# Sixteen places for the weight parts of the feed-forward layers, in tiles from the layers' own pools, with four smaller edits

## The chip, the core and the metric

The kernel runs on one core of a Trainium2 chip. The metric is the device time of one execution in microseconds (us); lower is better. TensorE (PE) multiplies, VectorE (DVE), ScalarE (ACT) and GpSimd (POOL) do the elementwise work, and SyncE (SP) issues nearly all DMAs.

## The reference, cut to what matters

A two-layer decoder trunk over 272 positions (16 learned ones and a sequence of 256), width 2048, in float32:

```python
for i in range(DEPTH):                       # 2 layers
    hn = rmsnorm(h, norm_mix[i])
    mix = mixer_ab(hn, ...) if i % 2 == 0 else mixer_cd(hn, ...)
    h = h + mix
    h = h + conv_ffn(rmsnorm(h, norm_ffn[i]), ffn_w_up[i], ffn_dw[i], ffn_w_down[i])
return rmsnorm(h, norm_final)[:, N_META:]

def mixer_ab(h, ...):
    a_val, a_gate, s_b, s_c, s_x = jnp.split(h @ w_in, ...)      # five parts, 1024 wide each
    a = silu(layernorm(causal_dwconv(a_val * sigmoid(a_gate), conf_dw) + conf_dw_b, ...))
    s = s_b * causal_dwconv(s_c * s_x, sc_dw)
    return jnp.concatenate([a, s], axis=-1) @ w_out

def conv_ffn(h, w_up, dw, w_down):           # D_FF = 5632
    u = causal_dwconv(h @ w_up, dw)          # width 3, over 2 * 5632 channels
    val, gate = u[..., :D_FF], u[..., D_FF:]
    return (jax.nn.silu(gate) * val) @ w_down
```

`mixer_cd` (gated linear attention and an RWKV-7 recurrence) is not touched by the change.

## The kernel before, in words

**Layout.** Channels lie on the 128 partitions and positions along the free axis, so the residual stream is 16 tiles `h[m]` of 128x272. A product with a weight matrix goes by output block: 128 output channels, the sum over k in steps of 128 input channels, in one PSUM tile.

**Split products.** Float32 products are made of rounded halves (type fp32r). For each group of `SUB = 4` steps of k, ACT casts the weights from the DMA'd tile `wf` to `wh` (L161), and DVE subtracts to give the rest, `wl` (L163). Then each k has three matmuls: `wh` with the high half of the moving operand (L181), `wh` with its low half (L182), `wl` with the high half (L183). In feed-forward layer 1 the up products work on 258 positions and use three forms of 260, 256 and 258 columns (L174 to L178). One output block of an up product has 16 steps of k, so 48 matmuls and four pairs of `wh` and `wl`; one of a down product, which is done in two halves of the 44 inner blocks, has 22 steps, so 66 matmuls. `wh` and `wl` are tiles of 128x512 elements, 2048 bytes per partition, in the pool `wpool`, five of each; since every tile of that pool is a multiple of 512 bytes long, all of them begin at the same remainder of 512 bytes. The moving operands have fixed places too: the normed input lies in `xslab` (`x`) and a second slab (`lt`), each half in a slot of `XW = 320` elements, where `make_x` writes them (L225 and L226), except ahead of `mixer_cd`, where the slots are 272 elements wide and so begin at several remainders of 256 bytes.

**Order.** A scheduler places the instructions of each engine from the order of the code and the tiles' dependences; the engines then run independently. A tile of a pool is free again when its last reader is done. The pools of the stages (`ab`, `ffn0`, `cd`, `ffn1`) are opened one after the other in the same memory.

**Between a mixer and its feed-forward layer.** Ahead of `ffn` the last products of the mixer are added to `h[m]` (`add_h`, L266), `make_x` writes the halves of the layer's input, and `feed` adds the squares into `nacc` (for the last block ACT squares, L240, and DVE adds, L241). `finish` sums `nacc` over the channels with a matmul against ones (L251) and gives 1/rms, `rstd`. The layer's products need only the halves, not `rstd`, which is multiplied in afterwards.

**The mixer of layer 0.** Its input product gives 40 blocks. Block triples of the short convolution part end in `sb = acc * rstd * cv`, whose halves are the moving operand `s_split` of `ab_out_s`; the last triple is ready only after the last block of the input product. Sums of squares `sums` give the mixer's `rstd`. A generator `ln_gen` gives the layer norm of the other part, a piece after each output block of `ab_out_s`.

**Start and end.** Two small constants for layer 1, `omm` and `omka`, are made by DVE (L1060, L1061). At the end 16 blocks `ob` are scaled (eleven by DVE from PSUM, five by POOL) and written out in eleven DMAs, all issued by SP (L1097).

Of the kernel before, what the change touches and what calls it, by code (L numbers as in the profile page):

```python
# [17 lines left out]
P = 128  # L18
# [4 lines left out]
KD = D // P  # L23
# [72 lines left out]
def _body(ctx, tc, nc, A):  # L96
# [53 lines left out]

    def gemm_steps(w, g, xs, kt, acc, pool_lo=(), load=LOADK):
        for k0 in range(0, kt, load):
# [3 lines left out]
            for s0 in range(0, nk, SUB):  # L156
                ns = min(SUB, nk - s0)
                src = wf[:, s0 * P:(s0 + ns) * P]
                wh = wpool.tile([P, SUB * P], F32R, tag="wh", name="wh")
                wl = wpool.tile([P, SUB * P], F32R, tag="wl", name="wl")  # L160
                last_hi[0] = S.copy(wh[:, :ns * P], src)  # L161
# [23 lines left out]

    def gemm(w, g, xs, n, pool_lo=()):
        acc = psA.tile([P, T], F32, tag="acc", name="acc")
        for _ in gemm_steps(w, g, xs, len(xs), acc[:, :n], pool_lo):
            tick()
        return acc[:, :n]  # L190
# [84 lines left out]
    def mixer_ab(tp):  # L275
# [79 lines left out]
        for i in range(8):  # L355
            ps3 = []
            for _ in range(3):
                ps3.append(gemm(A["ab_in"], g, xs, T, PLO))
                g += 1
                run_taps(NT)  # L360
                if len(ps3) == 1:
                    u = tp.tile([P, T], F32, tag="u0", name="u")
                    V.tensor_mul(u, ps3[0], nm.rstd)
                elif len(ps3) == 2:
                    u2 = tp.tile([P, T], F32, tag="u1", name="u2")
                    V.tensor_mul(u2, ps3[1], nm.rstd)
                    up = tp.tile([P, T + 2], F32, tag="up", name="up")
                    V.memset(up[:, 0:2], 0.0)
                    V.tensor_mul(up[:, 2:T + 2], u, u2)
                    cv = tp.tile([P, T], F32, tag="t2", name="cv")  # L370
                    conv3(cv, up, T, "sc_dw", i)
            sb = tp.tile([P, T], F32, tag="t3", name="sb")
            V.tensor_mul(sb, ps3[2], nm.rstd)
            V.tensor_mul(sb, sb, cv)
            d = halves[:, i]
            split(d, sb, T)
            s_split.append(parts(d, 0, T))
# [6 lines left out]
        def ln_gen():  # L384
# [5 lines left out]
            for i in range(8):  # L390
# [5 lines left out]
                if i % 2:  # L396
                    yield
            pv = psb()
            PE.matmul(pv[:, :T], ones, csum, start=True, stop=True)
# [13 lines left out]
        ln = ln_gen()  # L413
        next(ln, None)
        for m in range(KD):
            acc = gemm(A["ab_out_s"], m, s_split, T)
            h[m] = hpool.tile([P, T], F32, tag="h", name="h")
# [13 lines left out]
    def ffn(layer, nm, gname, c1, tp, feed, spill=None):  # L431
# [9 lines left out]
        for half in range(2):  # L441
            act = []
            for j in range(NFH):
                i = half * NFH + j
                res = []
                for q in range(2):
                    ps = gemm(up, 2 * i + q, xs, n + ex)
                    nm.finish()
# [15 lines left out]
            for m in range(KD):  # L464
                add_h(m, gemm(down, half * KD + m, act, no), T - no)
                if half:
# [592 lines left out]
    omka = cpool.tile([P, 16], F32, name="omka")[:, :8]  # L1059
    V.tensor_scalar(omm, par[:, PO["mu"]:PO["mu"] + 26], -1.0, 1.0, op0=ALU.mult, op1=ALU.add)  # L1060
    V.tensor_scalar(omka, par[:, PO["ka"]:PO["ka"] + 8], -1.0, 1.0, op0=ALU.mult, op1=ALU.add)  # L1061
    with tc.tile_pool(name="cd", bufs=2) as tp:
        nm = mixer_cd(tp, nm)
    with tc.tile_pool(name="ffn1", bufs=2) as tp:
# [25 lines left out]
        S.copy(rs, ps[:, :SEQ])  # L1090
        for a, b in ((0, 1), (1, 2), (11, 12), (2, 4), (12, 13), (4, 6), (13, 14), (6, 8), (14, 15), (8, 11), (15, 16)):
            for m in range(a, b):
                if m < 11:
                    V.tensor_mul(ob[:, m], ob[:, m], ps[:, :SEQ])
                else:
                    G.tensor_mul(ob[:, m], ob[:, m], rs)
            nc.sync.dma_start(A["outT"][:, a:b], ob[:, a:b])  # L1097

# [86 lines left out]
```

## Time and profile before

| | |
|---|---|
| time, median of 3 runs | 2460.76 us (2458.37 to 2470.93) |
| profiled execution, its own time | 2459.09 us |
| its span (first to last instruction) | 2457.3 us |
| PE busy | 2427.9 us, 99% of the span |
| DVE, ACT, POOL busy | 1794.0, 1338.9, 571.6 us |
| mean granted clock of TensorE | 0.997 of full speed |
| DMA | 423.95 MB, 173 GB/s over the span |

The span is measured on the chip by the profiler; the profiled execution's own time is 1.8 us longer and 1.7 us below the median of the timed runs. The stages follow one another: the mixer of layer 0 ends at about 348 us, feed-forward layer 0 at about 1130, the mixer of layer 1 at about 1701, and feed-forward layer 1 at about 2443 us. Matmuls are pipelined and overlap in the records: one has a duration of 0.28 us, but the next starts 0.12 us after it, so the distance from start to start (here called the spacing) is what a matmul costs while PE waits for nothing.

### The profile page before, as it was taken

How to read it: one execution, taken by the hardware profiler on the slowest of the kernel's cores; microseconds unless marked ns; L12 is line 12 of the kernel's file. 1: busy time of each engine (PE TensorE's matmuls, PEld its weight loads, DVE VectorE, ACT ScalarE, POOL GpSimd, SP SyncE). 2: the span in 40 equal slices, each digit the busy share in tenths (PEclk: the TensorE clock that was granted, in tenths of full speed). 3: DMA queues.
4: the chain of work that ended last, by engine and by line, in shares of the span. 5: the costliest groups of instructions: out<-in, count | busy, mean ns of one | idle time of the engine just before them, and what ended most of it. 6: DMA issues, size and time to landing. Idle time of an engine off the chain costs nothing.

```text
span 2457.3 us, 53575 instructions
## 1 busy us (share of the span) xinstructions
PE 2427.9 (99%) x20476; PEld 2371.8 (97%) x20476; DVE 1794.0 (73%) x3400; ACT 1338.9 (54%) x2573; POOL 571.6 (23%) x894
## 2 busy tenths in 40 slices
PE   8999999999999999999999999999999999999998
PEld 8999999999999999999999988899999999999997
DVE  8897897776556777667786678879777755777754
ACT  5444665555445555546745445546555545555653
POOL 5776140000000000121248044416110000101122
PEclk9999999999999999999999999999999999999999
DMA  6555555555665555665446342345555566555564
GB/s 223 191 176 180 172 173 180 181 178 173 181 183 179 178 177 180 181 196 190 142 148 179 126 130 84 101 131 179 188 184 188 183 191 197 187 184 186 179 198 147
DMA packets 130991, 423.95 MB, mean 173 GB/s; under 512 B 18832, under 2 KB 27216, under 8 KB 130736
## 3 DMA queue, kind: packets, MB, share of 16 engines
q1 hardware_dynamic: 129824, 417.99, 53.0%
q8 instruction: 161, 2.64, 0.4%
q0 software_dynamic: 912, 2.55, 0.4%
q14 instruction: 94, 0.77, 0.1%
HBM read 414.41 MB, written 5.93 MB: 171 GB/s over the span
## 4 chain that ended last, share of the span: by engine, by line
PE 97%; DVE 1%; ACT 0%; DMA 0%; issue 0%; POOL 0%; SPq 0%; DVEq 0%; POOLq 0%
PE acc L181 24%; PE acc L183 23%; PE acc L182 23%; PE acc L176 7%; PE acc L175 7%; PE acc L174 6%; PE ps L924 1%; PE ps L958 1%; PE ps L939 0%; PE acc L178 0%; PE ps L973 0%; PE ps L826 0%; PE ps L981 0%; PE ps L987 0%; DVE wl L163 0%
## 5 line engine op out<-in xcount | busy, mean ns | idle before, releaser
L161 ACT CAST wh<-wf 128x512 fp32r<-128x512 f32 (+1 forms) x1576 | 956.3, 611 | 876.4 <-PE acc L182 610.0
L163 DVE TENSOR_TENSOR wl<-wf,wh 128x512 fp32r<-128x512 f32 (+1 forms) x1465 | 1030.2, 708 | 462.6 <-ACT wh L161 417.0
L181 PE MATMUL acc<-x,wh 128*128 128x272 f32 (+2 forms) x2438 | 711.3, 292 | 1.4 <-ACT wh L161 1.4
L183 PE MATMUL acc<-x,wl 128*128 128x272 f32 (+2 forms) x2438 | 700.3, 287 | 1.0 <-DVE wl L163 0.9
L182 PE MATMUL acc<-x,wh 128*128 128x272 f32 (+2 forms) x2438 | 698.7, 287 | 0.0
L181 PEld LDWEIGHTS acc<-x,wh 128*128 128x128 f32 x2438 | 459.4, 188 | 15.7 <-issue 7.6
L183 PEld LDWEIGHTS acc<-x,wl 128*128 128x128 f32 x2438 | 459.7, 189 | 3.2 <-DVE wl L163 1.9
L182 PEld LDWEIGHTS acc<-x,wh 128*128 128x128 f32 x2438 | 459.9, 189 | 1.1 <-issue 0.3
L182 PE MATMUL acc<-act,wh 128*128 128x272 f32 (+1 forms) x1408 | 396.0, 281 | 0.0
L183 PE MATMUL acc<-act,wl 128*128 128x272 f32 (+1 forms) x1408 | 396.0, 281 | 0.0
L181 PE MATMUL acc<-act,wh 128*128 128x272 f32 (+1 forms) x1408 | 396.0, 281 | 0.0
L174 PE MATMUL acc<-x,wh 128*128 128x260 f32 x1144 | 323.6, 283 | 0.0
L176 PE MATMUL acc<-x,wl 128*128 128x258 f32 x1144 | 321.8, 281 | 0.0
L175 PE MATMUL acc<-x,wh 128*128 128x256 f32 x1144 | 321.0, 281 | 0.0
L181 PEld LDWEIGHTS acc<-act,wh 128*128 128x128 f32 x1408 | 264.7, 188 | 0.0
L183 PEld LDWEIGHTS acc<-act,wl 128*128 128x128 f32 x1408 | 264.7, 188 | 0.0
L182 PEld LDWEIGHTS acc<-act,wh 128*128 128x128 f32 x1408 | 264.7, 188 | 0.0
L175 PEld LDWEIGHTS acc<-x,wh 128*128 128x128 f32 x1144 | 215.6, 188 | 0.0
L174 PEld LDWEIGHTS acc<-x,wh 128*128 128x128 f32 x1144 | 215.5, 188 | 0.0
L176 PEld LDWEIGHTS acc<-x,wl 128*128 128x128 f32 x1144 | 215.3, 188 | 0.0
L163 POOL TENSOR_TENSOR wl<-wf,wh 128x512 fp32r<-128x512 f32 x111 | 149.0, 1350 | 55.9 <-ACT wh L161 54.8
L451 POOL MEMSET u<- 128x2 f32 x88 | 8.6, 101 | 572.9 <-DVE c L272 566.3
(334 smaller groups left out, 3740.5 us busy)
## 6 DMA issues: line engine op xcount, KB each, us to landing
wf<-up SPq DMA_DIRECT2D x352, 512.0 KB, 3.5
wf<-down SPq DMA_DIRECT2D x128, 512.0 KB, 3.8
wf<-cd_in SPq DMA_DIRECT2D x100, 512.0 KB, 3.6
wf<-ab_in SPq DMA_DIRECT2D x76, 512.0 KB, 3.6
wf<-down SPq DMA_DIRECT2D x64, 384.0 KB, 3.2
wf<-ab_out_s SPq DMA_DIRECT2D x16, 512.0 KB, 3.5
wf<-ab_out_a SPq DMA_DIRECT2D x16, 512.0 KB, 3.6
wf<-cd_out_o SPq DMA_DIRECT2D x16, 512.0 KB, 3.5
```

What stands on the lines that cost most here:

```text
L161: last_hi[0] = S.copy(wh[:, :ns * P], src)
L163: lo = eng.tensor_sub(wl[:, :ns * P], src, wh[:, :ns * P].bitcast(F32))
L174: PE.matmul(acc, a, x4, start=kk == 0, stop=False)
L175: PE.matmul(acc[:, 4:], a, x0, start=False, stop=False)
L176: PE.matmul(acc[:, 2:], b, x2, start=False, stop=False)
L181: PE.matmul(acc, a, xh, start=kk == 0, stop=False)
L182: PE.matmul(acc, a, xl, start=False, stop=False)
L183: PE.matmul(acc, b, xh, start=False, stop=kk == kt - 1)
L451: G.memset(u[:, 0:2], 0.0)
L924: PE.matmul(gv[:, :128], bkc, t[r, h0], start=True, stop=True)
L958: PE.matmul(wy[H[h0], 0:64], t[:, h0, 0:64], sv[:, h0], start=True, stop=True)
```

## The change

1. In both feed-forward layers `wh` and `wl` come from the layer's own pool `tp` in place of `wpool`. A tile is 64 elements wider (576), there are four of each in place of five, and the 512 elements used begin `4 * ((2*i+q) % 16)` elements into the tile for an up block and `4 * m` for a down block: sixteen places 16 bytes apart, one for each output block in turn.
2. The first three output blocks of `ab_out_s` get their accumulators together (two of `psA`, one of `psB`), and their products are issued as first and second block with k 0 to 3, first and second block with k 4 to 7, then the third. `ln_gen` has one more step.
3. `cv` is multiplied by `rstd` as soon as it is there, so that only one operation stands between the last block and `sb`.
4. `omm` and `omka` are placed behind the last `wl` of feed-forward layer 0.
5. The output is written in eleven DMAs with other borders: six issued by SP, five by ACT.

```diff
-    def gemm_steps(w, g, xs, kt, acc, pool_lo=(), load=LOADK):
+    def gemm_steps(w, g, xs, kt, acc, pool_lo=(), load=LOADK, wp=None):
...
-                wh = wpool.tile([P, SUB * P], F32R, tag="wh", name="wh")
-                wl = wpool.tile([P, SUB * P], F32R, tag="wl", name="wl")
+                if wp is None:
+                    wh = wpool.tile([P, SUB * P], F32R, tag="wh", name="wh")
+                    wl = wpool.tile([P, SUB * P], F32R, tag="wl", name="wl")
+                else:
+                    wh, wl = (wp[0].tile([P, SUB * P + 64], F32R, tag=n, name=n, bufs=4)[:, wp[1]:wp[1] + SUB * P]
+                              for n in ("wh", "wl"))
...
                     conv3(cv, up, T, "sc_dw", i)
+                    V.tensor_mul(cv, cv, nm.rstd)
             sb = tp.tile([P, T], F32, tag="t3", name="sb")
-            V.tensor_mul(sb, ps3[2], nm.rstd)
-            V.tensor_mul(sb, sb, cv)
+            V.tensor_mul(sb, ps3[2], cv)
...
+            yield
             pv = psb()
             PE.matmul(pv[:, :T], ones, csum, start=True, stop=True)
...
+        accs = [psA.tile([P, T], F32, tag="acc", name="acc") for _ in range(2)] + [psb()[:, :T]]
+        heads = [gemm_steps(A["ab_out_s"], m, s_split, 8, accs[m]) for m in range(3)]
+        for i in (0, 1, 0, 1):
+            next(heads[i])
         for m in range(KD):
-            acc = gemm(A["ab_out_s"], m, s_split, T)
+            if m == 2:
+                for _ in heads[2]:
+                    pass
+            acc = accs[m] if m < 3 else gemm(A["ab_out_s"], m, s_split, T)
...
-                    ps = gemm(up, 2 * i + q, xs, n + ex)
+                    ps = gemm(up, 2 * i + q, xs, n + ex, wp=(tp, 4 * ((2 * i + q) % 16)))
...
-                add_h(m, gemm(down, half * KD + m, act, no), T - no)
+                add_h(m, gemm(down, half * KD + m, act, no, wp=(tp, 4 * m)), T - no)
...
-    V.tensor_scalar(omm, par[:, PO["mu"]:PO["mu"] + 26], -1.0, 1.0, op0=ALU.mult, op1=ALU.add)
-    V.tensor_scalar(omka, par[:, PO["ka"]:PO["ka"] + 8], -1.0, 1.0, op0=ALU.mult, op1=ALU.add)
+    late = last_lo[0]
+    o1 = V.tensor_scalar(omm, par[:, PO["mu"]:PO["mu"] + 26], -1.0, 1.0, op0=ALU.mult, op1=ALU.add)
+    o2 = V.tensor_scalar(omka, par[:, PO["ka"]:PO["ka"] + 8], -1.0, 1.0, op0=ALU.mult, op1=ALU.add)
+    for o in (o1, o2):
+        behind(o, [late])
...
-        for a, b in ((0, 1), (1, 2), (11, 12), (2, 4), (12, 13), (4, 6), (13, 14), (6, 8), (14, 15), (8, 11), (15, 16)):
+        for a, b in ((0, 1), (11, 12), (1, 3), (12, 13), (3, 5), (13, 14), (5, 7), (14, 15), (7, 9), (15, 16), (9, 11)):
...
-            nc.sync.dma_start(A["outT"][:, a:b], ob[:, a:b])
+            (nc.sync if a < 11 else nc.scalar).dma_start(A["outT"][:, a:b], ob[:, a:b])
```

The change also moves instructions that the diff does not name. On PE, at the passage from the mixer of layer 0 to feed-forward layer 0, before (`acc_4706` is the last block of the mixer, `acc_4753` the first up block; between the two pieces stand the rest of that block's 48 matmuls):

```order
L182 MATMUL acc_4706<-halves_1482,wh_4725 128x272
L183 MATMUL acc_4706<-halves_1482,wl_4726 128x272
L181 MATMUL acc_4753<-x_80,wh_4756 128x272
L182 MATMUL acc_4753<-x_80,wh_4756 128x272
L183 MATMUL acc_4753<-x_80,wl_4757 128x272
...
L183 MATMUL acc_4753<-lt_4659,wl_4807 128x272
L251 MATMUL ps_4822<-nacc_4129,cst_79 128x272
L181 MATMUL acc_4835<-x_80,wh_4838 128x272
```

The same passage now (the lines of the code are four further down):

```order
L186 MATMUL acc_4706<-halves_1482,wh_4725 128x272
L187 MATMUL acc_4706<-halves_1482,wl_4726 128x272
L255 MATMUL ps_4822<-nacc_4129,cst_79 128x272
L185 MATMUL acc_4753<-x_80,wh_4756 128x272
L186 MATMUL acc_4753<-x_80,wh_4756 128x272
L187 MATMUL acc_4753<-x_80,wl_4757 128x272
```

The sum matmul of the norm has moved from behind the first up block to ahead of it. At the passage to feed-forward layer 1 the same has happened.

On ACT, at the same passage, before (`wh_4756` to `wh_4806` are the weights of the first up block, `wh_4838` to `wh_4919` belong to the second, the `lt` are the last three blocks of the layer's input):

```order
L161 CAST wh_4756<-wf_4754 128x512
L225 ACTIVATE lt_4659<-h_4008,par_78 128x272
L161 CAST wh_4772<-wf_4754 128x512
L161 CAST wh_4790<-wf_4788 128x512
L225 ACTIVATE lt_4659<-h_4050,par_78 128x272
L161 CAST wh_4806<-wf_4788 128x512
L161 CAST wh_4838<-wf_4836 128x512
L225 ACTIVATE lt_4659<-h_4087,par_78 128x272
L240 ACTIVATE nsq_4744<-h_4087 128x272
L161 CAST wh_4854<-wf_4836 128x512
```

And now, with the semaphores that each waits for in brackets (without numbers in the names; the first `CAST` is that of the first up block):

```order
L229 ACTIVATE lt<-h,par 128x272 [waits DVE_49] x3
L244 ACTIVATE nsq<-h 128x272 [waits Pool_49]
L165 CAST wh<-wf 128x512 [waits DMAHW4_49,PE_49]
L165 CAST wh<-wf 128x512
L165 CAST wh<-wf 128x512 [waits DMAHW5_49]
L165 CAST wh<-wf 128x512
L209 ACTIVATE sd<-ps,par 128x272
```

The casts of the first up block have moved from among the last `lt` to behind the last square, and the first of them waits for PE.

On DVE, from the last triple of the input product to `ab_out_s`, before (`wl_3513` is the third pair of weights of `ab_out_s`):

```order
L163 TENSOR_TENSOR wl_3484<-wf_3465,wh_3483 128x512
L373 TENSOR_TENSOR sb_3410<-acc_3341,rstd_392 128x272
L163 TENSOR_TENSOR wl_3513<-wf_3510,wh_3512 128x512
L374 TENSOR_TENSOR sb_3410<-sb_3410,cv_3337 128x272
L391 TENSOR_TENSOR conv_405<-conv_405,mu_3419 128x272
L391 TENSOR_TENSOR conv_660<-conv_660,mu_3419 128x272
L194 TENSOR_TENSOR halves_1482<-sb_3410,halves_1482 128x272
```

And now:

```order
L376 TENSOR_TENSOR cv_3337<-cv_3337,rstd_392 128x272
L167 TENSOR_TENSOR wl_3461<-wf_3424,wh_3460 128x512
L167 TENSOR_TENSOR wl_3477<-wf_3442,wh_3476 128x512
L378 TENSOR_TENSOR sb_3411<-acc_3342,cv_3337 128x272
L167 TENSOR_TENSOR wl_3513<-wf_3510,wh_3512 128x512
L395 TENSOR_TENSOR conv_405<-conv_405,mu_3419 128x272
L198 TENSOR_TENSOR halves_1482<-sb_3411,halves_1482 128x272
```

Between `sb` and the last `halves` one multiplication and one subtraction of `conv` fewer stand now.

## Rows read from the trace of the kernel before

**Rows 1.** The page: busy time by engine, and the chain that ended last.

```profile
PE 2427.9 (99%) x20476; PEld 2371.8 (97%) x20476; DVE 1794.0 (73%) x3400; ACT 1338.9 (54%) x2573; POOL 571.6 (23%) x894
PE 97%; DVE 1%; ACT 0%; DMA 0%; issue 0%; POOL 0%; SPq 0%; DVEq 0%; POOLq 0%
```

**Rows 2.** Waits of PE: us in total, times, longest.

```profile
PE ps L251 <- DVE sum L307: 2.1, 1, 2.1
PE acc L182 <- DVE halves L194: 1.9, 1, 1.9
```

**Rows 3.** Stretches: length, busy (records) of PE, PEld, DVE, ACT, POOL, PEclk, DMA, GB/s.

```profile
500.00:620.00 120.00, 120.00 (x975) 120.00 (x974) 84.02 (x151) 67.09 (x123) 9.69 (x29) 1.00 0.54 175
1990.00:2006.00 16.00, 16.00 (x144) 16.00 (x143) 8.81 (x15) 8.02 (x14) 0.00 (x0) 1.00 0.69 199
```

**Rows 4.** Timeline of PE, mixer of layer 1: start, us, what.

```profile
1273.93 0.28 PE L183 MATMUL acc<-x,wl 128*128 128x272 f32 x1
...
1277.92 0.29 PE L182 MATMUL acc<-x,wh 128*128 128x272 f32 x1
```

**Rows 5.** Timeline of PE, first and last matmul of two up blocks, layer 1.

```profile
1804.77 0.28 PE L174 MATMUL acc<-x,wh 128*128 128x260 f32 x1
...
1810.31 0.28 PE L178 MATMUL acc<-lt,wh 128*128 128x260 f32 x1
1810.43 0.28 PE L174 MATMUL acc<-x,wh 128*128 128x260 f32 x1
...
1816.04 0.28 PE L178 MATMUL acc<-lt,wh 128*128 128x260 f32 x1
```

**Rows 6.** The page, costliest groups: busy and mean ns, idle before and its releaser.

```profile
L161 ACT CAST wh<-wf 128x512 fp32r<-128x512 f32 (+1 forms) x1576 | 956.3, 611 | 876.4 <-PE acc L182 610.0
L163 DVE TENSOR_TENSOR wl<-wf,wh 128x512 fp32r<-128x512 f32 (+1 forms) x1465 | 1030.2, 708 | 462.6 <-ACT wh L161 417.0
```

**Rows 7.** Timeline of PE from the mixer to feed-forward layer 0.

```profile
348.60 0.28 PE L183 MATMUL acc<-halves,wl 128*128 128x272 f32 x1
348.72 0.29 PE L181 MATMUL acc<-x,wh 128*128 128x272 f32 x1
...
354.64 0.62 PE L251 MATMUL ps<-nacc,cst 128*128 128x272 f32 x2
```

**Rows 8.** Timelines of DVE and ACT there.

```profile
349.13 0.42 DVE L266 TENSOR_TENSOR h<-h,acc 128x272 f32<-128x272 f32 x1
...
350.57 0.43 DVE L241 TENSOR_TENSOR nacc<-nacc,nsq 128x272 f32<-128x272 f32 x1
...
350.02 0.42 ACT L240 ACTIVATE nsq<-h 128x272 f32<-128x272 f32 x1
```

**Rows 9.** Waits of POOL: the first tile of a feed-forward layer's pool.

```profile
POOL u L451 <- PE ps L251: 6.7, 1, 6.7
```

**Rows 10.** Timelines of PE and DVE from the mixer to feed-forward layer 1.

```profile
1701.53 0.28 PE L183 MATMUL acc<-ysp,wl 128*128 128x258 f32 x1
...
1703.46 0.42 DVE L241 TENSOR_TENSOR nacc<-nacc,nsq 128x258 f32<-128x258 f32 x1
```

**Rows 11.** A wait of PE early in mixer 1, and stretches behind three waits.

```profile
1158.95 0.39 PE L181 MATMUL acc<-x,wh 128*128 128x272 f32 x1 [1.43 <-ACT wh L161]
...
31.40:35.40 4.00, 4.00 (x31) 3.92 (x32) 3.97 (x4) 2.07 (x4) 3.24 (x3) 1.00 0.71 250
256.20:260.20 4.00, 4.00 (x33) 4.00 (x34) 4.00 (x8) 2.32 (x5) 1.55 (x3) 1.00 0.36 118
1159.70:1163.00 3.30, 3.30 (x13) 2.98 (x14) 2.83 (x6) 3.24 (x8) 0.00 (x0) 0.50 0.56 173
```

**Rows 12.** Timeline of DVE ahead of the sum of mixer 0's norm.

```profile
28.50 1.25 DVE L1060 TENSOR_SCALAR omm<-par 128x26 f32<-128x26 f32 x1
```

**Rows 13.** The end: SP's issues of the output, and a stretch as in rows 3.

```profile
2448.28 5.24 SPq L1097 DMA_DIRECT2D outT<-ob  x11
...
2451.00:2455.00 4.00, 0.00 (x0) 0.00 (x0) 0.21 (x1) 0.00 (x0) 0.00 (x0) 0.50 1.01 370
```

More of the change, by code (lines that the diff above doesn't have):

```diff
@@ L184, in gemm_steps, with gemm @@
                 yield
-    def gemm(w, g, xs, n, pool_lo=()):
+    def gemm(w, g, xs, n, pool_lo=(), wp=None):
         acc = psA.tile([P, T], F32, tag="acc", name="acc")
-        for _ in gemm_steps(w, g, xs, len(xs), acc[:, :n], pool_lo):
+        for _ in gemm_steps(w, g, xs, len(xs), acc[:, :n], pool_lo, wp=wp):
             tick()
```

## The prediction

> **What bounds the kernel now.** I read the busy line and the chain first [rows 1]: PE is busy for 99% of the span, and 97% of the chain that ended last is PE. So time is won only in two ways: PE waits less, or a matmul costs less. The waits of PE come next; the change touches two of them, 2.1 and 1.9 us long [rows 2]. Then the spacing, read as the length of a stretch over the matmuls that start in it (a stretch lists two or three records that began ahead of it, which I take off). In feed-forward layer 0, with 272 columns, it is 120 / 973 = 123.3 ns; in the down products of layer 1, with 256 columns, 16 / 141.5 = 113.1 ns [rows 3]. [...] The mixer of layer 1, with 272 columns again but moving operands at several places, has 32 steps in 3.99 us, 124.7 ns [rows 4]. And two neighbouring up blocks of layer 1, equal but for the block, have 47 steps in 5.54 and in 5.61 us, 117.9 and 119.4 ns [rows 5]. So something besides the columns sets the spacing, by a per cent or so, and it changes with the tiles. DVE and ACT are no bound in the feed-forward layers: they work 70% and 56% of such a stretch [rows 3].
>
> **The places of the weights (part 1).** The layers have 6336 matmuls of 272 columns, 4224 of 256 to 260 (up, layer 1) and 2112 of 256. No row shows weights at sixteen places; the nearest rows bound it.
> Cost: if 272 columns go to the spacing of the mixer, +1.4 ns x 6336 = +8.9 us; if all up blocks of layer 1 go from their mean (about 118.8, between the two of [rows 5]) to the slow one, +0.6 x 4224 = +2.5; if 256 columns pay what the slow up block pays, 119.4 less 0.8 for two columns, +5.5 x 2112 = +11.6. Together +23.
> [...]
> I take +4.5: half of the mixer's surplus on the 272 columns, because that row is the nearest (same shape, only the places mixed, there of the moving side), half because a block now keeps one place from its first matmul to its last; nothing for the rest, whose rows speak both ways.
> [...]
>
> **Four tiles deep (part 1).** ACT's casts wait for PE to free a tile, 610 us in all [rows 6], so tiles are made as early as their number allows. One tile lasts 12 x 123.3 = 1.48 us. A tile freed by PE needs a cast (0.61) and a subtraction (0.71) [rows 6], 1.3 us, before PE comes back to it; with four tiles that is three tiles later, 4.4 us. The remaining 3.1 us cover an operation or two of DVE or ACT in between. Cost nothing; without that cover, at most some tenths of a us per late tile.
>
> **The passages into the feed-forward layers (part 1, in the order only).** The weights' tiles now lie in the memory that the pool of the stage before used, so the first of them must wait until that pool's last reader is done. That reader is the norm's sum over `nacc`; before, POOL's first tile of such a pool waited for just this matmul [rows 9], but no weights did. In the order of the changed kernel the sum stands ahead of the first up block, and the first cast waits for PE. The chain that used to run beside 48 up matmuls now stands bare.
> Passage 0 [rows 7, 8]: the last product starts at 348.60 and its addition to `h` ends at 349.55; ACT's halves and square end at 350.44; DVE's addition into `nacc` ends at 351.00. Then the sum (0.62), the cast (0.61), and two hops of some 0.06 (an estimate, from the gap between 350.44 and 350.57): the first up matmul starts at about 352.35 instead of 348.72, 3.6 us late. The third matmul waits for `wl`, 0.71 after the cast against two matmuls, +0.45; the sum saves about as much where it stood [rows 7]. Passage 1 [rows 10]: `nacc` ends at 1703.88, the first up matmul starts at 1705.25 instead of 1701.64, 3.6 us. Together **+7.2**.
> Behind it ACT casts four tiles and DVE subtracts them in 0.61 and 0.71 us each against 1.48 of PE, so nothing else runs late; `rstd` comes earlier than before. On SP only the loads of `wf` are queued, and they are ahead.
> [...] I take one such stretch each, **+3.4**; bounds 0 and twice that.
>
> **The smaller parts.** `omm` and `omka` (1.25 us [rows 12] and a tenth) leave DVE ahead of the last addition of the sums, for which PE waits 2.1 [rows 2]: **-1.2**. They go behind the last `wl` of layer 0, where nothing waits for them.
> `ab_out_s`: PE waits 1.9 us for the last halves [rows 2]. Now the second block's first 12 matmuls (1.48 us) come ahead of that point, and one multiplication and one subtraction fewer stand ahead of the halves in DVE's order. The wait goes, **-1.9**; next late could be the third block's `wl`, behind three subtractions, so the low end is -1.
> The end: eleven issues take SP 5.24 us, about 0.48 each [rows 13]. By issues alone five on ACT would save up to 1.8 us; but the DMA engines are full for the last four of these microseconds (share 1.01), so only what was idle ahead of that comes back: **-0.7**.
>
> **Sum.** 2459.1 + 7.2 + 3.4 - 1.2 - 1.9 - 0.7 = 2465.9 with the places at nothing, and with +4.5 for them 2470.4, on the profiled execution's own time, which lies 1.7 under the median of the runs and 0.7 over the fastest. I say **2470**.
>
> **Rivals.**
> A. The sixteen places cost as much as the mixed rows or more: 2465.9 + 9 to 23 = 2475 to 2489, **slower**. [...] Against it: nothing is mixed within a block. It decides from a mean spacing of 124.4 ns in layer 0.
> [...]
> C. Places change nothing: 2466. For it: weights and moving operand may not meet at all; the spacings of [rows 4, 5] differ in the moving side. [...]
> D. The change doesn't lengthen the passages (the cast waits, but for an event long past): 2459.1 - 3.8 and the places, 2455 to 2460. For it: a wait in an order says nothing of its length. Against it: the sum itself has moved ahead of the first up block, and that needs `nacc`.
>
> **How the numbers follow.** Forecast (2467 to 2474) 0.33; A 0.29; B 0.14; C 0.14; D 0.10. 0.5%, about what a measurement of this kernel can tell from no change, is 12.3 us: faster is below 2448.5, slower above 2473.1. Faster: most of B, 0.13. Slower: A and somewhat over a third of the forecast, 0.41. Same: the rest, 0.46. The range reaches to the upper end of A and over two thirds of B: **2448 to 2489**. It leaves out the better third of B, some 0.05, and up to 0.1 for places that cost more than any of these rows.
>
> **What would show it.** In the changed kernel's profile: two waits of PE for ACT's `wh` of 0.7 us and two for the sum of about 2.2, at 349 to 352 and at 1702 to 1705, or one of them named for both; a stretch at 0.50 behind each; no wait for `halves`; a wait for the sum early on of about 0.9 instead of 2.1; issues on ACT's queue at the end with the DMA share as full as now. [...] I would be wrong if the places move the spacing by more than the rows of this trace span, or if PE waits for weights inside the layers, which would show four tiles to be too few.

## The result and the profile after

The changed kernel takes 2498.37 us (median of 3 runs, 2494.26 to 2500.46) against 2460.76 before; the ratio is 1.0149, with a 95% interval of 1.0132 to 1.0166. It is slower by 37.6 us, 9 us above the range. Its profiled execution is the fastest of the three, 2494.26 us with a span of 2492.4; the sums below are made between the two profiled executions, 35.2 us apart in time and 35.1 in span.

Between which points the 35.1 us arise, read from the same events in both timelines:

| from | to | before | after | difference of the piece |
|---|---|---|---|---|
| start | last matmul of mixer 0 starts | 348.60 | 347.11 | -1.5 |
| there | first up matmul of layer 0 | 348.72 | 351.20 | +4.0 |
| there | last matmul of mixer 1 | 1701.53 | 1721.70 | +17.7 |
| there | first up matmul of layer 1 | 1701.64 | 1725.31 | +3.5 |
| there | last addition to `h` | 2443.49 | 2479.37 | +12.2 |
| there | end of the span | 2457.3 | 2492.4 | -0.8 |

**The passages** first. The waits of PE (us in total, times, longest):

```profile
PE ps L255 <- DVE nacc L245: 3.9, 2, 2.0
PE acc L185 <- ACT wh L165: 3.1, 3, 1.5
PE ps L255 <- DVE sum L311: 1.3, 1, 1.3
...
PE acc L178 <- ACT wh L165: 0.7, 1, 0.7
```

The two waits for `nacc` are new; the one for the sum was 2.1 and is 1.3, the one for `halves` is gone [rows 2]. The timelines of PE, DVE and ACT at the first passage, to be read beside [rows 7, 8] (start, us, what, and in brackets the wait):

```profile
347.11 0.28 PE L187 MATMUL acc<-halves,wl 128*128 128x272 f32 x1
349.36 1.13 PE L255 MATMUL ps<-nacc,cst 128*128 128x272 f32 x2 [1.97 <-DVE nacc L245]
351.20 0.59 PE L185 MATMUL acc<-x,wh 128*128 128x272 f32 x1 [0.71 <-ACT wh L165]
...
348.87 0.43 DVE L245 TENSOR_TENSOR nacc<-nacc,nsq 128x272 f32<-128x272 f32 x1
...
350.53 2.18 ACT L165 CAST wh<-wf 128x512 fp32r<-128x512 f32 x4 [1.79 <-PE ps L255]
```

ACT stands for 1.79 us and then casts four tiles in one go; what it waits for is the sum matmul (`PE ps L255`), as the order said. Between 347.11 and 351.20 lie 4.1 us where one spacing of 0.12 stood, so 4.0 us are lost. In both passages the granted clock falls to 0.50 of full speed (from 351 to 356 and from 1726 to 1728 us); stretches behind them (columns as in [rows 3]):

```profile
351.50:355.00 3.50, 3.50 (x15) 3.27 (x15) 3.50 (x5) 2.21 (x5) 0.00 (x0) 0.50 0.38 122
355.00:358.00 3.00, 3.00 (x21) 3.00 (x20) 1.49 (x3) 0.62 (x1) 0.00 (x0) 0.77 0.57 210
1725.50:1729.00 3.50, 3.50 (x17) 3.28 (x18) 3.50 (x5) 2.31 (x5) 0.00 (x0) 0.57 0.32 96
```

The first up block therefore has a mean spacing of 179.8 ns in layer 0 and 154.6 in layer 1, against 125.3 and 118.3 of the other blocks at the same place: 47 steps, +2.6 and +1.7 us. Not all of it is the clock. The third matmul needs the first `wl`, and from the start of the first matmul at 351.20 to that of the fourth pass 1.12 us, three steps, where one step at 0.50 is 0.23, as between these two:

```profile
352.32 0.43 PE L185 MATMUL acc<-x,wh 128*128 128x272 f32 x1
352.55 0.43 PE L186 MATMUL acc<-x,wh 128*128 128x272 f32 x1
```

That is 0.4 us more than three such steps, and 0.5 in the same way in layer 1, so the clock itself cost 3.4 of the 4.3 us.

**The spacing** carries most of the rest. The same stretch of layer 0 as in [rows 3], and one of the down products of layer 1:

```profile
500.00:620.00 120.00, 120.00 (x958) 120.00 (x957) 83.73 (x150) 65.95 (x120) 9.71 (x30) 1.00 0.53 174
1980.00:2090.00 110.00, 110.00 (x933) 110.00 (x933) 59.22 (x103) 51.83 (x90) 0.73 (x1) 1.00 0.64 185
```

958 records where 975 were, at full clock and with no wait: 125.5 ns instead of 123.3; and 110 / 930.5 = 118.2 instead of 113.1. Two neighbouring blocks of those products, at the fifth and the sixth place (timeline of PE, first and last matmul of each, 65 steps):

```profile
2009.82 0.28 PE L185 MATMUL acc<-act,wh 128*128 128x256 f32 x1
...
2017.18 0.28 PE L187 MATMUL acc<-act,wl 128*128 128x256 f32 x1
2017.30 0.28 PE L185 MATMUL acc<-act,wh 128*128 128x256 f32 x1
...
2025.03 0.28 PE L187 MATMUL acc<-act,wl 128*128 128x256 f32 x1
```

7.36 / 65 = 113.2 and 7.73 / 65 = 118.9 ns: the same shapes, engines and cast times, only the weights 16 bytes further on. Done for every block in this way, each place gives the same spacing whenever it comes round, in ns (within 0.1, but for four blocks: the first of each layer, at half clock, and the third and fourth of layer 0, which ran at 126.6 and 126.7). The column `~258` stands for the products of 256 to 260 columns:

```
place     up, 272   down, 272   up, ~258   down, 256
 1         125.3      126.7      118.3      120.0
 2         125.0      125.0      120.1      118.3
 3         125.3      126.6      118.7      118.3
 4         124.4      126.7      117.8      117.8
 5         123.4      123.3      119.4      113.4
 6         126.7      126.7      119.9      118.8
 7         123.4      123.4      118.0      117.3
 8         126.7      126.7      119.4      119.8
 9         126.6      126.6      118.7      118.6
10         123.5      123.4      119.9      119.8
11         126.6      126.6      119.2      120.0
12         126.7      126.7      119.9      118.1
13         126.7      126.7      118.4      117.9
14         125.8      125.8      120.3      116.7
15         125.7      125.8      118.4      116.7
16         126.6      125.1      118.0      117.3
mean       125.5      125.7      119.0      118.1
before     123.3      123.3      118.8      113.3
```

The fifth place has the remainder of 256 bytes that all weights had before. With 4224, 2112, 4224 and 2112 matmuls the means, before rounding, cost 9.2 + 5.0 + 1.1 + 9.9 = **25.2 us**.

**The end.** SP's issues, ACT's, and a stretch:

```profile
2483.64 4.33 SPq L1112 DMA_DIRECT2D outT<-ob  x6
...
2483.96 3.61 ACTq L1112 DMA_DIRECT2D outT<-ob  x5
...
2486.00:2488.00 2.00, 0.00 (x0) 0.00 (x0) 0.89 (x3) 0.00 (x0) 0.66 (x1) 0.50 1.03 364
```

The issues go out side by side, the DMA engines are as full as before (1.03 against 1.01), and 0.8 us are saved.

### The profile page after: what moved, and what is told of

Read it like the earlier page. It is cut to its first block, busy times and chain, and to the rows that moved or that the text cites. A ratio compares the mean times of both kernels' runs of the same rounds, so it can differ in the third digit from the quotient of the medians.

```text
span 2492.4 us, 53139 instructions
## 1 busy us (share of the span) xinstructions
PE 2457.8 (99%) x20476; PEld 2399.1 (96%) x20476; DVE 1792.5 (72%) x3400; ACT 1341.2 (54%) x2573; POOL 573.2 (23%) x894
## 4 chain that ended last, share of the span: by engine, by line
PE 96%; DVE 2%; ACT 1%; DMA 1%; POOL 0%; issue 0%; SPq 0%; DVEq 0%; ACTq 0%; POOLq 0%
PE acc L185 24%; PE acc L187 23%; PE acc L186 23%; PE acc L180 7%; PE acc L179 7%; PE acc L178 6%; PE ps L936 1%; PE ps L970 1%; PE ps L951 0%; PE acc L182 0%; PE ps L985 0%; PE ps L838 0%; PE ps L993 0%; DVE wl L167 0%; PE ps L999 0%
## 5 line engine op out<-in xcount | busy, mean ns | idle before, releaser
L185 PE MATMUL acc<-x,wh 128*128 128x272 f32 (+2 forms) x2438 | 713.5, 293 | 2.2 <-ACT wh L165 2.2
L187 PE MATMUL acc<-x,wl 128*128 128x272 f32 (+2 forms) x2438 | 702.7, 288 | 1.0 <-DVE wl L167 1.0
L186 PE MATMUL acc<-x,wh 128*128 128x272 f32 (+2 forms) x2438 | 700.8, 288 | 0.0
L185 PEld LDWEIGHTS acc<-x,wh 128*128 128x128 f32 x2438 | 459.5, 188 | 17.1 <-issue 8.0
L187 PEld LDWEIGHTS acc<-x,wl 128*128 128x128 f32 x2438 | 459.6, 189 | 3.5 <-DVE wl L167 2.1
L186 PEld LDWEIGHTS acc<-x,wh 128*128 128x128 f32 x2438 | 460.2, 189 | 1.1 <-issue 0.3
L186 PE MATMUL acc<-act,wh 128*128 128x272 f32 (+1 forms) x1408 | 400.7, 285 | 0.0
L187 PE MATMUL acc<-act,wl 128*128 128x272 f32 (+1 forms) x1408 | 400.7, 285 | 0.0
L185 PE MATMUL acc<-act,wh 128*128 128x272 f32 (+1 forms) x1408 | 400.6, 285 | 0.0
L185 PEld LDWEIGHTS acc<-act,wh 128*128 128x128 f32 x1408 | 265.1, 188 | 0.0
L187 PEld LDWEIGHTS acc<-act,wl 128*128 128x128 f32 x1408 | 265.0, 188 | 0.0
L186 PEld LDWEIGHTS acc<-act,wh 128*128 128x128 f32 x1408 | 265.0, 188 | 0.0
```

What stands on the lines that cost most here:

```text
L185: PE.matmul(acc, a, xh, start=kk == 0, stop=False)
L186: PE.matmul(acc, a, xl, start=False, stop=False)
L187: PE.matmul(acc, b, xh, start=False, stop=kk == kt - 1)
```

## The experiments

The indented text of each is what was expected before it ran.

**One place.** Everything of the change, but each block at the fifth place.

```diff
-                    ps = gemm(up, 2 * i + q, xs, n + ex, wp=(tp, 4 * ((2 * i + q) % 16)))
+                    ps = gemm(up, 2 * i + q, xs, n + ex, wp=(tp, 16))
...
-                add_h(m, gemm(down, half * KD + m, act, no, wp=(tp, 4 * m)), T - no)
+                add_h(m, gemm(down, half * KD + m, act, no, wp=(tp, 16)), T - no)
```

> The changed kernel with every block of both feed-forward layers at the fifth place (16 elements into the tile), the same remainder of 256 bytes as in the kernel before; pools, depth and passages stay as changed. Theory P (the places carry 25.6 of the 35.2 us that the profiled executions differ by): the spacings go back to 123.3, about 118.8 (up to 119.4) and 113.4 ns, and the profiled time falls from 2494 to about 2469, that is 8 to 12 us over the kernel before, the passages alone less the small savings. Rival D (the layers' own pools or four tiles instead of five carry the loss): the time stays within some 3 us of 2494 and the spacings stay at 126, 119 and 118.

Measured 2471.19 us (median; 2467.60 to 2475.82), ratio to before 1.0038 (1.0022 to 1.0053). The blocks are back at 123.3, 118.8 and 113.4 ns; layer 0 in its profile:

```profile
500.00:620.00 120.00, 120.00 (x975) 120.00 (x974) 85.78 (x154) 66.89 (x122) 9.78 (x30) 1.00 0.50 177
```

So 27 of the 37.6 us, by the medians, belong to the sixteen places and not to the pool or its depth; the passages stay.

**The small edits only.** The weights of the feed-forward layers come from `wpool` again.

```diff
-                    ps = gemm(up, 2 * i + q, xs, n + ex, wp=(tp, 4 * ((2 * i + q) % 16)))
+                    ps = gemm(up, 2 * i + q, xs, n + ex)
...
-                add_h(m, gemm(down, half * KD + m, act, no, wp=(tp, 4 * m)), T - no)
+                add_h(m, gemm(down, half * KD + m, act, no), T - no)
```

> The changed kernel with the feed-forward weights from the common pool again, five deep, at one place; the four smaller edits stay. Theory P: the passages' waits (2.0 and 0.7 us, twice) and the stretches at half clock behind them go, the spacings are those of before, and what stays is the small savings as the trace of the changed kernel shows them: 1.5 us in the first mixer and 0.8 at the end, so a profiled time of about 2456.8 and a ratio of 0.999. Rival S (one of the smaller edits costs something that the other parts hid): 2459 or more.

Measured 2456.54 us (2455.52 to 2460.99), ratio 0.9978 (0.9968 to 0.9989): 0.2% better than the kernel before, 2.4 us between the profiled executions. The passages show no wait, since the first cast no longer needs the memory of the stage before. What parts this kernel from the one with one place is the price of the passages with their clock: 14.7 us by the medians, where the trace of the changed kernel shows 4.0 + 3.5 + 2.6 + 1.7 = 11.8. Their two profiled executions are 17.1 us apart. Of these, 9.8 lie in the passages and the layers, and 7.6 in the two mixers, whose code is the same in both (0.4 go off at the end). With one place PE waited longer there, 2.4 us for the sum and 2.6 for a cast, than the 1.2 and 1.3 with the small edits only (us in total, times, longest):

```profile
PE acc L185 <- ACT wh L165: 4.2, 3, 2.6
PE ps L255 <- DVE sum L311: 2.4, 1, 2.4
```

Behind both waits the granted clock fell to 0.50, and with the small edits it stayed at 1.00 (0.995 and 0.998 on the mean of the profiled executions). So a part of the 14.7 us may lie in the mixers and not in the passages; why those two waits were longer, the runs don't show.

**Four tiles in all stages.** As the last, with `bufs=4` for `wh` and `wl`.

> As the run with the small edits only, but four tiles of each kind of weight part in place of five, in all stages. Theory P: four are enough, PE waits for no weights inside the feed-forward layers, the time is within 1 us of that run. Rival D: PE waits for wl or wh inside the layers and the time is 3 us or more above it.

Measured 2467.32 us (one run): theory P fell, though not where the change uses four tiles. In the feed-forward layers all spacings are those of five tiles and PE waits for no weights. The loss is in the mixers, 1.6 us in that of layer 0 and 9.4 in that of layer 1 by the profiled executions, where PE's waits are now (us in total, times, longest):

```profile
PE acc L185 <- ACT wh L165: 4.0, 3, 2.9
PE acc L187 <- DVE wl L167: 2.2, 5, 0.8
```

The small edits alone have 2.2 and 0.9 there. Behind the wait of 2.9 at 1158.95 the clock falls, as it did in [rows 11]:

```profile
1157.00:1162.00 5.00, 3.05 (x12) 2.82 (x13) 3.94 (x9) 3.84 (x8) 0.89 (x2) 0.61 0.28 76
```

**What the spacing hangs on: the moving side.** The small edits, with the down products' moving operand 64 bytes lower and no weight moved.

```diff
-ACT_GAP = 48
+ACT_GAP = 28
```

> The small edits only, with the gap ahead of the down products' moving operands cut from 48 to 28 elements, so that those lie 64 bytes lower and the weights stay where they were. Theory R (what counts is where the weights lie relative to the moving operand): the down products run as the ninth place did, 126.6 ns in layer 0 and 118.6 in layer 1, some 18 us more in all; the up products stay. Theory A (the weights' own address counts, or that of the writes of casts and subtractions): the down products stay at 123.3 and 113.3 ns and the time at 2456.8.

Measured 2479.01 us (one run). All down blocks of layer 0 are at 126.7 ns and all of layer 1 at 118.7, the numbers of the ninth place (126.6 and 118.6); the up products did not move. In layer 0 nine of the sixteen places had 126.6 or 126.7, so the match says more in layer 1. The weights lay as before and their matmuls were slower by 3.4 and 5.4 ns with the other operand moved. So it isn't the weights' own address alone. Of the 22.5 us by which this run lies above the small edits, 18.2 are in the two layers, as expected; 4.7 are in the mixer of layer 0, where PE waited 3.3 us for the sum and the granted clock was 0.99.

**What it hangs on: the writes.** The changed kernel, in which the feed-forward layers read four fixed tiles of each kind.

```diff
-                    wh, wl = (wp[0].tile([P, SUB * P + 64], F32R, tag=n, name=n, bufs=4)[:, wp[1]:wp[1] + SUB * P]
-                              for n in ("wh", "wl"))
...
+                    wh, wl = (t[(k0 + s0) // SUB % 4][:, wp[1]:wp[1] + SUB * P] for t in wp[0])
```

> The changed kernel in which the feed-forward layers load, cast and subtract no weights: four fixed tiles of each kind, filled once with constants, are read at the sixteen places in turn. Left out: the layers' true weights, so the numbers are not the reference's. Theory R (TensorE's own two reads, of the weights and of the moving operand, get in each other's way): the spacing follows the place as in the changed kernel, block by block, means 125.7, 119.1 and 118.0 ns. Theory W (the reads meet the writes of casts, subtractions and DMAs): the spacing is flat over the places, at 123.3 and 113.3 or below.

Measured 2501.09 us (one run). The spacing of every place is that of the table, within 0.1 ns, but for the first block of each layer. A stretch of layer 0, and one of the down products of layer 1:

```profile
500.00:620.00 120.00, 120.00 (x958) 120.00 (x957) 33.32 (x70) 18.97 (x40) 9.73 (x30) 1.00 0.00 1
1990.00:2100.00 110.00, 110.00 (x934) 110.00 (x933) 6.03 (x15) 0.00 (x0) 0.00 (x0) 1.00 0.00 1
```

958 records again in the first, with ACT and DVE at less than half their work and no DMA (share 0.00). In the second ACT and POOL do nothing and DVE is busy for 6 of the 110 us, and the spacing is still 118.1 ns on the mean. Theory W fell: what makes the difference lies in PE's own work. That it is its two reads, as theory R says, is what is left of the two; PE's writes of the sums were not tried apart.

**The two kinds apart.** `wh` at the fifth place, `wl` at the first.

```diff
-                    wh, wl = (wp[0].tile([P, SUB * P + 64], F32R, tag=n, name=n, bufs=4)[:, wp[1]:wp[1] + SUB * P]
-                              for n in ("wh", "wl"))
+                    wh, wl = (wp[0].tile([P, SUB * P + 64], F32R, tag=n, name=n, bufs=4)[:, o:o + SUB * P]
+                              for n, o in (("wh", 16), ("wl", 0)))
```

> The changed kernel with all wh at the fifth place (that of before) and all wl 64 bytes lower, at the first (126.7 ns in the down products of layer 0, 120.0 in those of layer 1, when both parts lay there). Theory R, in the form that a weight load is slowed by the matmul beside which it runs: one of the three matmuls of each k is long and two are as before, so a mean of 123.3 + 1.1 = 124.4 ns in layer 0 and 113.4 + 2.2 = 115.6 in the down products of layer 1. If instead the loads disturb every matmul alike or not at all: 126.7 and 120, or 123.3 and 113.4.

Measured 2486.07 us (one run). Down products of layer 0: 124.4 ns, as expected, but of the three matmuls of a k none is "as before": the steps after L185, L186 and L187 take 125.8, 120.0 and 127.6. Layer 1: 117.8, where 115.6 was expected, all three steps alike (117.5, 118.3, 117.5). The simple form of theory R, one slow load beside one matmul, falls.

**Finer, and apart by other distances.** The fixed tiles again, at 64 places 4 bytes apart, and with `wl` at eight other distances from `wh`.

> The fixed weight tiles again (the feed-forward layers' true weights are left out), now at 64 places 4 bytes apart, a step for each up block, and 32 places 8 bytes apart for the down blocks. Theory R with lines of 16 bytes (only the 16-byte place counts): four neighbouring places have one spacing, that of their multiple of 16 bytes. Rival: the spacing changes with every 4 bytes, and places between may be better than 123.3, 117.8 and 113.3 ns.

> The fixed weight tiles again (the feed-forward layers' true weights are left out), with wh at the sixteen places and wl at another place than wh, by 32 to 224 bytes, eight differences for the layer with 272 columns. Theory R (each weight load meets the moving operand that streams beside it, and the two kinds of load add up): spacings lie between those of the two places, and none is under the best of the common places, 123.3 ns (272 columns) and 113.3 (256). Rival: some pairs of places are better than any common place, towards the 120.0 ns that one of the three matmuls showed when wl lay 64 bytes below wh; that would be worth up to 3.3 ns x 6336 = 21 us.

Measured 2497.11 and 2500.49 us (one run each). The spacing changes from one 4-byte step to the next (layer 0, from 56 bytes on: 123.4, 125.1, 123.4, 126.6, 123.7, 123.3, 126.7), so lines of 16 bytes are not the unit. And no place and no pair is under 123.3 (272 columns), 113.4 (256) or 117.6 (up products of layer 1). None of the places tried is a gain for layer 0: the kernel before was at the lowest of them already. One thing didn't fit: the down products of layer 1 at the fifth place ran at 117.8 here and at 113.4 in the run before with the same tiles.

**A better place for one stage.** The small edits, all weights in wider common tiles (four deep), those of the up products of layer 1 at the fourth place.

> The small edits; all weight parts in the common pool, four deep, in tiles 64 elements wider, at the remainder of before, except the up products of layer 1, whose weights lie 240 bytes further on (the remainder of the fourth of the sixteen places, which had the lowest spacing of that stage, 117.8 ns). Theory P: up products of layer 1 at 117.8 instead of 118.8 ns on the mean, 4224 matmuls, so 4.2 us less than the run with the small edits: about 2452.6. Rival (the 117.8 belonged to the layer's own pool and not to the place): the stage stays at 118.8 and the time at 2456.8; with four tiles too few, more.

Measured 2462.74 us (2461.00 to 2469.16). The stage itself does what was expected, 851 records in a stretch in which 844 were in the kernel before, 117.7 ns, -4.4 us. But the mixers pay for four tiles as above.

**The same by the moving operand.** Five tiles, weights as before; the input halves of layer 1 lie 16 bytes higher (first) or 16 bytes lower by the remainder of 256 (second).

```diff
+            e = 4 if self.c0 and self.wide and self.g == "norm_ffn1" else 0
-            x = slab[:, 2 * w * i:2 * w * (i + 1)].rearrange("p (a t) -> p a t", a=2)
+            x = slab[:, 2 * w * i + e:2 * w * (i + 1) + e].rearrange("p (a t) -> p a t", a=2)
```

> The small edits only, weights five deep at the remainder of before; the moving operand of the up products of layer 1 lies 4 elements (16 bytes) further on in its slab, so that the weights stand to it as at the fourth of the sixteen places. Theory R (the relative place counts): these products go to 117.8 ns from a mean of 118.8, 4224 of them, 4.2 us less than the run with the small edits: about 2452.3, and the mixers keep their time, since five tiles stay. Theory A (the weights' own address counts): no change, 2456.5.

> The small edits only, weights five deep at the remainder of before; the moving operand of the up products of layer 1 lies 60 elements (240 bytes) further on, which is 16 bytes lower by the remainder of 256. After the shift by 16 bytes upward gave 119.9 ns, what the sixth place gave, the mirrored theory M (a shift of the moving operand acts as the same shift of the weights would) expects the 117.8 ns of the fourth place: 4.2 us less than the run with the small edits, about 2452.3. Theory R (the opposite shift) expects the 119.9 of the sixth place: 4.6 us more, about 2461. If neither holds, both starts count by themselves, and the spacing may be anything from 117.6 to 121.

Measured 2462.17 us (2460.26 to 2470.12) and 2472.21 (2470.52 to 2475.00). The up products run at 119.9 and 120.1 ns: both theories about the relative place fall, for steps of 16 bytes. The second has a surprise a stage further on. A stretch of the down products of layer 1, first and second kernel:

```profile
1965.00:2060.00 95.00, 95.00 (x841) 95.00 (x840) 52.98 (x90) 44.51 (x77) 0.00 (x0) 1.00 0.67 192
```

```profile
1965.00:2060.00 95.00, 95.00 (x809) 95.00 (x808) 51.09 (x87) 43.05 (x75) 0.00 (x0) 1.00 0.65 189
```

113.3 and 117.8 ns. By their code, which differs only in where the input of the up products lies, all 2112 of these matmuls read the same addresses and write the same PSUM tiles in both programs, in the same order. Only what ran ahead of them differs.

**How the stream comes in.** The second of these kernels, with a small matmul ahead of each feed-forward block.

```diff
+                if cols and k0 + s0 == 0:
+                    PE.matmul(psb()[:, :cols], wh[:, :P], xs[0][0][:, :cols], start=True, stop=True)
```

> The kernel of the last run (moving operand of the up products of layer 1 16 bytes lower), with one more small matmul ahead of each feed-forward output block, into a PSUM tile that nobody reads: 8 to 176 columns ahead of the up blocks, 8 to 256 ahead of the down blocks, a different number for each block in turn. In the last run the down products of layer 1 ran at 117.8 ns, although each of their matmuls reads and writes the same addresses as in the run before it (x 16 bytes higher), where they ran at 113.3. Theory H (equal addresses allow several spacings, and how the stream comes into a block decides which it keeps): spacings now differ from block to block at equal places, the down products of layer 1 show both 113.3 and 117.8, and some blocks of layer 0 may leave 123.3. Rival (the spacing belongs to the addresses, and something else differed between those runs): one spacing for each stage, as in the last run; the added matmuls cost about 240 x 0.05 = 12 us in either case.

Measured 2500.71 us (one run). Two neighbouring down blocks of layer 1 (timeline of PE; 51 and 50 steps):

```profile
1979.51 0.28 PE L188 MATMUL acc<-act,wh 128*128 128x256 f32 x1
...
1985.29 0.28 PE L188 MATMUL acc<-act,wh 128*128 128x256 f32 x1
...
1987.04 0.28 PE L187 MATMUL acc<-act,wh 128*128 128x256 f32 x1
...
1992.93 0.28 PE L189 MATMUL acc<-act,wl 128*128 128x256 f32 x1
```

5.78 / 51 = 113.3 and 5.89 / 50 = 117.8 ns. Past its first few matmuls each of the 32 blocks is at one of these two values, 11 at the first and 21 at the second; in layer 0 the blocks are at 123.3 or 126.7, in the up products of layer 1 at 117.8 or 119.9. Each number of columns gives the same value each time it comes round in the up products of layer 1. Theory H holds: equal addresses allowed two spacings each here, and the entry into a block decided which one it kept to its end.

The kernel before had shown a sign of it. The two blocks of [rows 5] are followed by a third at 119.1 ns and a fourth that is back at 117.9 (first and last matmul of each, 47 steps):

```profile
1816.16 0.28 PE L174 MATMUL acc<-x,wh 128*128 128x260 f32 x1
...
1821.76 0.28 PE L178 MATMUL acc<-lt,wh 128*128 128x260 f32 x1
1821.88 0.28 PE L174 MATMUL acc<-x,wh 128*128 128x260 f32 x1
...
1827.42 0.28 PE L178 MATMUL acc<-lt,wh 128*128 128x260 f32 x1
```

From the third on, all the up blocks of each half go round in these three values. Nothing that their matmuls read or write has a period of three: all read the same input, the accumulators are two, and a block takes four weight tiles of five. With four tiles in place of five the three values come round in the same way. That fits theory H, with something that passes from one block to the next.

## Why the prediction was wrong

**The bound and what to look at** were right: PE's waits, its clock and the spacing are what moved, and the waits and the stretches at 0.50 that it named are what the profile shows. The spacing follows the place, in a pattern of sixteen blocks.

**The passages** were right: +7.2 forecast, +4.0 and +3.5 measured, through the mechanism named, the first cast behind the sum; half a us between the two is the sum's matmul, 1.13 us at the first passage, where the granted clock was 0.52 from 349.5 to 350.5, and 0.70 at the second, where it was 1.00. The +3.4 for PE's clock was the author's estimate, twice the loss of the one stretch at 0.50 in [rows 11]; no run shows that a wait has to bring such a stretch (behind waits of 2.1 and 1.9 us the clock was 1.00 in the kernel before), and what the two passages showed is 3.4 us lost to the clock in the first blocks. Another 0.9 there is the wait around the first `wl`, which the prediction had set off against the sum.

**Four tiles** cost nothing in the layers, as argued. That the mixers need five is shown by the two kernels with four there (1.6 and 9.4 us lost in the two mixers of the first); the change leaves them five.

**The smaller parts** were forecast at -3.8 and gave -2.3. The end is right (-0.7 against -0.8). The issues that moved to ACT would by the prediction's own figure be 5 x 0.48 = 2.4 us and not 1.8, but its term didn't use that. The sum's wait shrank by 0.8, not 1.2. The wait for `halves` (1.9) went, but the low end of that term came true, by another wait than the one named: PE stands 0.90 us for a `wh` of `ab_out_s`. Its cast stands on ACT behind a square of the layer norm, and that one waited for POOL:

```profile
259.60 0.43 ACT L397 ACTIVATE sq<-conv 128x272 f32<-128x272 f32 x1 [0.29 <-POOL csum L399]
259.94 0.60 ACT L165 CAST wh<-wf 128x512 fp32r<-128x512 f32 x1
...
260.54 0.36 PE L185 MATMUL acc<-halves,wh 128*128 128x272 f32 x1 [0.90 <-ACT wh L165]
```

**The places** are the step that failed: taken at +4.5, measured at +25.2. Three things were wrong in it. The upper bound of the 272-column products was the mixer's 124.7 ns; thirteen of the sixteen places lie above it in the down products, at up to 126.7, so that term is +14.2 where its bound was +8.9. The 256-column products were given nothing, though their bound (+11.6) was nearly what they paid (+9.9). They stood at the fewest ns per column of all (113.3 / 256 = 0.443, against 0.453 with 272 and 0.460 in the up products of layer 1), so they had more to lose than the others; that should have decided the term, and no place of the sixteen was better than 113.4. The 0.8 ns for two columns in that bound no run shows at full clock. At 0.50 the first blocks took 226.7 ns with 272 columns (352.55 to 353.91, six steps) and 215.0 with 258 on the mean (1726.42 to 1727.71); halved for full clock that is 0.8 for two columns, an estimate from these two. The bound had 5.5 ns a matmul in all, and the runs showed 9.9 / 2112 = 4.7. Third, half a bound was taken because a block keeps one place, but a block that keeps a bad one pays it 48 or 66 times. The prediction's own sign of being wrong, places that move the spacing by more than the rows span, is what came. And it read the 117.9 and 119.4 ns of [rows 5] as the doing of the tiles, where three values come round in turn at equal places. Rival A was the right one, with 0.29; its upper end of 2489 fell short by 2.2 us of places, 1.5 us of small savings that did not come, about one of the clock, and the 4 us by which the median of the runs lies above the profiled execution. The 0.14 for places that gain (B), and the lower end of the range with it, rested on the author's estimate of a time for the columns alone, which no run shows; of the places tried none was under 123.3 ns with 272 columns.

**Rival C**, places change nothing, fell as well: the run with fixed weights (no cast, DMA share 0.00, the same 958 records) and the one that moved only the other operand show that at equal columns the spacing moves with the places of what PE reads, by up to 6.7 ns (113.3 to 120.0). No other engine is needed for it: with ACT and POOL at nothing and DVE at 6 of 110 us the mean was still 118.1.

**Open** is the mechanism under it. Shown are that both operands' places and the entry into the block matter; why 113.3 and 117.8, and what carries from block to block, isn't. No run moved the accumulators in PSUM; the two that the blocks use in turn show no difference in the kernel before (123.3 or 123.4 ns for the blocks of layer 0). The places of the changed kernel may act through the entry, through the addresses, or both; e.g. the 256-column products also have values between these two, at 116.7 and 117.3.

## What to carry to other kernels

The place of an operand was not neutral here, by up to 6.7 ns a matmul: read the spacing per shape and per block. The shape with the fewest ns per column (0.443, down products of 256 columns) lost the most by the sixteen places, 4.7 ns on the mean against 2.2 and 2.4 with 272 columns and 0.3 in the up products of layer 1, and of the down products with 272 columns thirteen of sixteen places were worse by 1.7 ns and more. Weight tiles from a stage's own pool, in memory that the stage before used, put the first cast behind that stage's last reader (ACT stood for 1.79 us at the first passage): look in the order for what has moved ahead of the first matmul, and sum the chain that then stands bare. The edits around it, here four small ones, are worth a kernel of their own: they alone gave 2456.54 us, ratio 0.9978.

## What the hardware showed that I had not expected

A stream of weight loads and matmuls with the same addresses in the same order ran at one of two spacings (113.3 or 117.8 ns with 256 columns, 123.3 or 126.7 with 272), and a single small matmul ahead of a block decided which one it kept, past its first few matmuls, to its end. Over the down products of layer 1 that is 4.5 ns x 2112 = 9.5 us, which came or went with an edit a stage earlier that touched none of these matmuls.
